# Moving the prompt's down-projection into the sample's seven block products, in a tuned fp32 encoder kernel

## The chip, the core and the metric

The kernel runs on one core of a Trainium2 chip. A core has a matrix engine (PE; its weight loads are shown apart as PEld), a vector engine (DVE), a scalar engine (ACT), a general engine (POOL) and a queue that issues the transfers (SP). The metric is the device time of one execution in microseconds; the lower, the better. Times are medians of several executions, and one more execution was recorded by the hardware profiler. Names such as L816 are lines of the kernel before, unless the text says that they are the changed kernel's.

## The reference, cut to what matters

Two batches go through one encoder layer with the same weights: a prompt of 512 tokens and a sample of 1024 tokens, both 1024 wide.

```python
h = rmsnorm(x, norm_attn_g)
z = h @ w_in                              # q, k, v and the two halves of a gated convolution
a_out = window_attention(q, k, v, bias, sink)          # |q - k| <= 128, 8 heads in 2 groups
c = silu(layernorm(dwconv31(ca * sigmoid(cb))))
x = x + concat(a_out, c) @ w_out
h = rmsnorm(x, norm_ffn_g)
u = dwconv3(h @ w_up)                     # 1024 -> 2 * 2816
x = x + (silu(u[..., :2816]) * u[..., 2816:]) @ w_down # 2816 -> 1024
y = rmsnorm(x, norm_final_g)
```

In the attention, with a sink logit `sk` for each head, `m = max(max(sc), sk)`, `p = exp(sc - m)` and the denominator is `sum(p) + exp(sk - m)`.

## The kernel before

Everything is fp32. A matmul operand is split in two rounded parts, `hi = round(x)` by a cast on ACT and `lo = x - hi` by a subtraction on POOL or DVE, and a product is made of three matmuls: hi·hi, hi·lo and lo·hi. So one "matmul of the algorithm" is three of the profile, nearly all of them 128x128 weights against 512 columns.

The program is emitted as one long list and then ordered by a scheduler that replays it against its own timeline; for each engine the result is one fixed order. What stands beside what is set while emitting: a main line of projections calls `tick()` after a few matmuls, and `tick()` advances two side queues by rates. `side` holds generators for the attention and the output projection (rates `RA` to `RE`), `convs` and `late` hold the taps of the 31-wide convolution, 0.66 credits each (rates `CA`, `CB`, `CL`, `CLO`, `CD`). From the last step of the sample's up-projection on, PE and SP are ordered by hand: they run in the order of the program text.

The stages, in order of time:

1. The prompt's and the sample's input projections (L250 to L253), with the prompt's attention, its convolution and its output projection (L641 to L643) from the side queues, to about 350 us.
2. The prompt's feed-forward layer in 22 steps of 128 hidden channels each (`ffn_step`). A step makes the gate half and the value half (8 chunks of three matmuls each, L250 to L253, 48 matmuls), evacuates them with ACT (L779) and two three-tap passes on DVE each (L775), and gates them: tanh on ACT (L793), `(t + 1) * a` on DVE (L794), times the value on DVE or POOL (L795), then the split (L797, L798). Every second step the down-projection `down` of two steps runs: for 4 token tiles and 2 column halves, six matmuls (L813 to L815) and an addition into the residual on DVE (L816). `w_down` is loaded (L750) and split (L143, L144) for this. Beside it, `side` runs the whole attention of the sample (16 units of four heads: scores L502, reduction L505, softmax L512 to L519, transposes L546, values L560 and L561), and `late` runs the sample's convolution (L293).
3. The sample's output projection (L641 to L643) and the sums for the next stage.
4. The sample's up-projection as a block algorithm with seven products instead of eight (Winograd's form of Strassen's): tokens, channels and columns are cut in halves, L1045 to L1047. The gated values of each pair of hidden blocks and their sums go to DRAM, seven tensors `ga[i, p]` for each of 11 pairs `p` (L1183 to L1198).
5. The sample's down-projection by the same seven products, `ORDER = (1, 2, 5, 6, 7, 4, 3)`: a product `i` is summed over the 11 pairs; a step loads `ga[i, p]` and a block of `w_down` (L1308), forms the block's difference, splits both, and runs 12 matmuls (4 token tiles, L1354 to L1356) into two wide banks of PSUM of 128x1024. At the end of a product the banks are evacuated and combined (`evacuate`). The last product is cut so that its tiles finish one after another (`finish`: sum of squares on ACT, reciprocal root on POOL, scale and store).

PSUM has four wide banks in stage 5, so that with two for each product the next product begins in the other two.

## Time and profile before

| | before |
|---|---|
| median of 3 runs | 1562.63 us (1561.66 to 1564.55) |
| the profiled execution | 1563.92 us, span 1562.1 us |
| PE busy in the span | 1519.2 us, 6909 matmuls and transposes |
| DVE busy | 1200.5 us |
| ACT busy | 799.2 us |
| POOL busy | 729.5 us |
| moved by DMA | 207.62 MB, 133 GB/s |

"Busy" is the time in which an instruction of the engine was under way. The matmuls of PE overlap: one lasts some 0.39 us, and the next starts 0.23 us after it. A view by windows gives the busy time of each engine in a stretch of the span, with the number of instructions behind an x. A view by groups gives the count, the total and the mean in ns of one instruction of a line, then the idle time of the engine just ahead of them and what ended it.

### The profile page before, as it was taken

The numbers are of one execution on the slowest core, as the hardware profiler recorded it, in microseconds if no ns is written. First come the engines' busy times: TensorE is split into PE (matmuls) and PEld (weight loads), VectorE is DVE, ScalarE is ACT, GpSimd is POOL, SyncE is SP. The second block draws the span as 40 slices with busy tenths as digits, with TensorE's granted clock in tenths as the row PEclk, the third lists the DMA queues.
The fourth block names the chain that finished last, engine by engine and source line by source line (L and its number), as shares of the span: only waits on it lengthen the run. The fifth ranks groups of instructions, "written<-read, shape, count | busy, mean of one in ns | idle before, by whom it ended". The sixth has DMA issues, their size and how long they took to land. (4 is left out here: it accounts for less than half of the span.)

```text
span 1562.1 us, 20200 instructions
## 1 busy us (share of the span) xinstructions
PE 1519.2 (97%) x6909; PEld 1234.5 (79%) x6909; DVE 1200.5 (77%) x1731; ACT 799.2 (51%) x1426; POOL 729.5 (47%) x559
## 2 busy tenths in 40 slices
PE   8899899999998999999999999999999999999998
PEld 6787788887886778888877887888888878788886
DVE  7999868638989996756675768777777777877795
ACT  4634566335565655656554455444444445544364
POOL 7651344238576676656653324555555554000135
PEclk9999999999999999999999999999999999999999
DMA  7573246446331333333657222333333332694642
GB/s 229 157 201 95 87 118 165 130 133 166 108 117 64 108 108 109 99 97 95 212 164 230 82 68 78 111 102 101 101 102 102 101 102 101 206 354 144 219 142 108
DMA packets 209771, 207.62 MB, mean 133 GB/s; under 512 B 11156, under 2 KB 150748, under 8 KB 209541
## 3 DMA queue, kind: packets, MB, share of 16 engines
q1 hardware_dynamic: 209669, 206.35, 42.0%
q8 instruction: 54, 0.88, 0.2%
q14 instruction: 48, 0.39, 0.1%
HBM read 158.84 MB, written 48.51 MB: 133 GB/s over the span
## 5 line engine op out<-in xcount | busy, mean ns | idle before, releaser
L144 POOL TENSOR_TENSOR q<-q,q 128x1024 fp32r<-128x1024 f32 x72 | 175.0, 2436 | 68.8 <-ACT q L143 33.8
L921 POOL TENSOR_TENSOR q<-q,q 128x512 fp32r<-128x512 f32 x82 | 114.0, 1401 | 155.9 <-ACT q L1031 151.4
L250 PE MATMUL u<-h,q 128*128 128x512 f32 x400 | 158.5, 396 | 3.6 <-DVE h L775 2.8
L251 PE MATMUL u<-h,q 128*128 128x512 f32 x400 | 158.6, 396 | 0.6 <-DVE h L212 0.6
L253 PE MATMUL u<-h,q 128*128 128x512 f32 x384 | 151.9, 396 | 2.2 <-POOL q L144 2.2
L1045 PE MATMUL w<-h,q 128*128 128x512 f32 x372 | 147.4, 396 | 3.1 <-ACT h L1126 1.7
L1047 PE MATMUL w<-h,q 128*128 128x512 f32 x372 | 145.9, 392 | 0.6 <-POOL q L921 0.6
L293 DVE SCALAR_TENSOR_TENSOR c<-c,cvw,c 128x512 f32<-128x512 f32 x184 | 138.1, 750 | 2.4
L1046 PE MATMUL w<-h,q 128*128 128x512 f32 x350 | 137.6, 393 | 0.0
L143 ACT CAST q<-q 128x1024 fp32r<-128x1024 f32 x72 | 75.6, 1050 | 77.5 <-POOL q L144 44.6
L918 POOL TENSOR_TENSOR q<-q,q 128x1024 f32<-128x1024 f32 x8 | 23.8, 2989 | 182.9 <-DVE q L918 171.2
L250 PE MATMUL b<-h,q 128*128 128x512 f32 x256 | 102.1, 399 | 2.9 <-DVE d L323 2.9
L1354 PE MATMUL w<-h,h 128*128 128x512 f32 x264 | 103.8, 393 | 0.0
L1356 PE MATMUL w<-h,h 128*128 128x512 f32 x264 | 103.6, 392 | 0.0
L921 DVE TENSOR_TENSOR h<-h,h 128x512 fp32r<-128x512 f32 (+1 forms) x128 | 92.3, 764 | 11.4 <-ACT h L925 9.2
L251 PE MATMUL b<-h,q 128*128 128x512 f32 x256 | 100.7, 393 | 0.0
L253 PE MATMUL b<-h,q 128*128 128x512 f32 x256 | 100.5, 393 | 0.0
L1355 PE MATMUL w<-h,h 128*128 128x512 f32 x244 | 95.9, 393 | 0.0
L921 POOL TENSOR_TENSOR c<-q,c 128x512 fp32r<-128x512 f32 x46 | 71.0, 1557 | 51.8 <-ACT c L1031 51.8
L250 PEld LDWEIGHTS u<-h,q 128*128 128x128 f32 x400 | 75.6, 189 | 20.4 <-DVE h L775 3.3
L925 ACT CAST h<-h 128x512 fp32r<-128x512 f32 x101 | 58.7, 618 | 59.4 <-DVE h L921 27.0
L251 PEld LDWEIGHTS u<-h,q 128*128 128x128 f32 x400 | 75.5, 189 | 16.4 <-DVE h L212 1.6
(457 smaller groups left out, 4278.8 us busy)
## 6 DMA issues: line engine op xcount, KB each, us to landing
q<-in_w_up SPq DMA_DIRECT2D x88, 512.0 KB
h<-in_w_down SPq DMA_DIRECT2D x90, 256.0 KB
ga<-q SPq DMA_DIRECT2D x64, 256.0 KB
h<-ga SPq DMA_DIRECT2D x57, 256.0 KB
q<-in_w_in SPq DMA_DIRECT2D x28, 512.0 KB
q<-in_x_sample SPq DMA_DIRECT2D x15, 512.0 KB
h<-qsd SPq DMA_DIRECT2D x24, 256.0 KB
q<-ga SPq DMA_DIRECT2D x20, 256.0 KB
```

The lines of the kernel that those rows point to most:

```text
L144: (nc.vector if dve else nc.gpsimd).tensor_tensor(lo[:], raw[:], hi[:].bitcast(F32), op=ALU.subtract)
L250: nc.tensor.matmul(out, whi[:, kc, :], hi[:], start=(kc == 0), stop=False)
L251: nc.tensor.matmul(out, whi[:, kc, :], lo[:], start=False, stop=False)
L253: nc.tensor.matmul(out, wlo[:, kc, :], hi[:], start=False, stop=(kc == KC - 1))
L293: nc.vector.scalar_tensor_tensor(acc[:], src(t), w(t), acc[:], op0=ALU.mult, op1=ALU.add)
L921: (eng or nc.vector).tensor_tensor(out, a, b, op=ALU.subtract)
L1045: nc.tensor.matmul(out, whi[:, s], hi[:], start=(start and c == 0), stop=False, **go)
L1046: nc.tensor.matmul(out, whi[:, s], lo[:], start=False, stop=False, **go)
L1047: nc.tensor.matmul(out, wlo[:, s], hi[:], start=False, stop=(stop and c == 3), **go)
L1354: nc.tensor.matmul(out, sh[:, c], th[:], start=(p == 0), stop=False)
L1355: nc.tensor.matmul(out, sh[:, c], tl[:], start=False, stop=False)
L1356: nc.tensor.matmul(out, sl[:, c], th[:], start=False, stop=(p == NPAIR - 1))
```

## The change

The prompt's down-projection no longer runs inside stage 2. `ffn_step` ends with `gate`, which writes the gated values of the prompt to DRAM in the form that the seven products need: tokens in two halves of 256, hidden blocks in pairs, seven tensors `gb[i, p // 2]` that hold two pairs each. For that it makes four sums of 128x256 for each pair, three on DVE and one on POOL, and 17 of the 22 products with the value half are on POOL (6 before). `w_down` is neither loaded nor split in stage 2, and there is no addition into the residual; the residual of the prompt goes to DRAM (`x1d`, four more tensors).

In stage 5 a step now serves six token tiles: the four of the sample and two of the prompt (`w = 2`), against the same split block of `w_down`. There are three wide banks for each product, `trio` instead of `pair2`, and the order within a product runs its first two and its last two pairs bank by bank. The last product runs the prompt's tiles along with the sample's first two; the prompt's four output blocks are finished there.

The softmax works on negated scores: the reduction (L505) yields `-(sc + bias)` and its minimum, begun from `-sk`, so that the two small DVE operations after it (L512, L513) are gone; the exponentials take scale -1, and the sink's exponential is made for one head at a time on ACT.

The rates of the side queues are other ones (`RD`, `RN`, `CL`, `CLO`, `CD`), and the sample's attention is queued at step 1 instead of step 3 (`U0`).

```diff
-RA, RB, RBO, RD, RN, RE = 1.2, 0.8, 2.5, 0.52, 0.8, 0.9
+RA, RB, RBO, RD, RN, RE = 1.2, 0.8, 2.5, 0.78, 0.95, 0.9
-CL, CLO, CD = 0.5, 0.6, 0.65
+CL, CLO, CD = 0.7, 0.7, 0.6
-U0 = 3
+U0 = 1
...
-                out=p[:, :nk], in0=sc[:, :nk], in1=bias[h][:, off:off + nk], scale=1.0,
-                scalar=-3.0e38, op0=ALU.add, op1=ALU.max, accum_out=mx[:, j:j + 1])
+                out=p[:, :nk], in0=sc[:, :nk], in1=bias[h][:, off:off + nk], scale=-1.0,
+                scalar=nsink[:, h:h + 1], op0=ALU.add, op1=ALU.min, accum_out=negm[:, j:j + 1])
...
-        nc.vector.scalar_tensor_tensor(negm[:], mx[:], -1.0, nsink[:, hs], op0=ALU.mult, op1=ALU.min)
-        nc.vector.tensor_tensor(es[:], sinkb[:, hs], negm[:], op=ALU.add)
         for j in range(GRP):
-            nc.scalar.activation(pr[j][:, :nk], pr[j][:, :nk], AF.Exp, bias=negm[:, j:j + 1],
+            nc.scalar.activation(pr[j][:, :nk], pr[j][:, :nk], AF.Exp, scale=-1.0, bias=negm[:, j:j + 1],
                                  accum_out=den[:, j:j + 1])
-        nc.scalar.activation(es[:], es[:], AF.Exp)
+        for j in range(GRP):
+            h = kv * GRP + j
+            nc.scalar.activation(es[:, j:j + 1], sinkb[:, h:h + 1], AF.Exp, bias=negm[:, j:j + 1])
...
+    def gate(j, a, b):
+        t = sb.tile([NT])
+        nc.scalar.activation(t[:], a[:], AF.Tanh, scale=0.5)
+        nc.vector.scalar_tensor_tensor(t[:], t[:], 1.0, a[:], op0=ALU.add, op1=ALU.mult)
+        (nc.vector if j % 4 == VG else nc.gpsimd).tensor_tensor(t[:], t[:], b[:], op=ALU.mult)
+        p = j // 2
+        if j % 2 == 0:
+            even_p[p] = t
+            store_gb(1, p, t[:, HL])
+            return
+        e, x, y = even_p.pop(p), sb.tile([NT]), sb.tile([HT])
+        store_gb(2, p, t[:, HL])
+        store_gb(4, p, t[:, HR])
+        eng = nc.vector
+        eng.tensor_tensor(x[:, HR], e[:, HR], t[:, HR], op=ALU.add)
+        store_gb(5, p, x[:, HR])
+        nc.gpsimd.tensor_tensor(x[:, HL], e[:, HL], e[:, HR], op=ALU.subtract)
+        store_gb(7, p, x[:, HL])
+        eng.tensor_tensor(e[:, HR], x[:, HR], e[:, HL], op=ALU.subtract)
+        store_gb(6, p, e[:, HR])
+        eng.tensor_tensor(y[:], t[:, HL], e[:, HR], op=ALU.subtract)
+        store_gb(3, p, y[:])
...
+        if p % 2 == 0:
+            g = pr.pop((("g", i, 0), p // 2))
+            n = slice(0, min(2, NPAIR - p) * HT)
+            hi, lo = hp[i, p // 2] = sb.tile([NT], F32R), sb.tile([NT], F32R)
+            nc.scalar.copy(hi[:, n], g[:, n])
+            sub(lo[:, n], g[:, n], hi[:, n].bitcast(F32))
...
     def mm_down(out, i, p, tt):
         (sh, sl), (th, tl) = hl[i, p]
-        c = slice(tt * P, (tt + 1) * P)
+        if tt < 4:
+            c = slice(tt * P, (tt + 1) * P)
+        else:
+            sh, sl = hp[i, p // 2]
+            c0 = (p % 2) * HT + (tt - 4) * P
+            c = slice(c0, c0 + P)
...
+    def group(i, p, w, lead=LEAD):
+
+        k = ORDER.index(i) * NPAIR + p
+        if len(pr) < CAP and sum(f[0][0] == "h" for f in sb.free) > ROOM:
+            load_next(1)
+        make(k + lead)
+        if w not in pd:
+            pd[w] = wide()
+        for q in range(2):
+            mm_down(pd[w][:, q * NT:(q + 1) * NT], i, p, 2 * w + q)
...
+    def product(i):
+        rest = [(p, w) for p in range(2, NPAIR - 2) for w in range(NW3)]
+        if i == 1:
+            order = [(1, 0), (1, 1), (0, 2), (1, 2)]
+        else:
+            order = [(p, w) for w in range(NW3) for p in range(2)]
+        order += rest + [(p, w) for w in range(NW3) for p in (NPAIR - 2, NPAIR - 1)]
+        for p, w in order:
+            group(i, p, w)
...
+    done_at = {1: 4, 3: 5, 4: 0, 6: 1, 7: 2, 9: 3}
+    for p, w in [(0, 2), (1, 2), (0, 0), (1, 0)] + [(p, w) for p in range(2, NPAIR) for w in (2, 0)]:
+        last_group(p, w)
+        if w == 0 and p in done_at:
+            tt = done_at[p]
+            finish(4 + tt if tt < 4 else tt - 6, (cut(u, tt), cut(e, tt)), False)
+    for tt in (4, 5, 0, 1):
+        add(cut(o12, tt), zs[tt // 2][:, (tt % 2) * NT:(tt % 2 + 1) * NT], cut(o12, tt))
+        finish(tt if tt < 4 else tt - 8, (cut(o11, tt), cut(o12, tt)), False)
```

How the order of the engines changes is shown at three places. A row is an instruction with its line, what it writes and reads, and the shape that it writes; the letter ahead of a tile's number is its kind of buffer (h 128x512 and q 128x1024 in SBUF, c a padded convolution row or the convolution's PSUM bank, s small, and a, b, u, w banks of PSUM).

First, DVE in the middle of the feed-forward layer. Before, in one step (L775 the three-tap passes, L816 the additions of the down-projection, L293 convolution taps, of which only the first of a run is shown, L549 splits of transposed attention weights, L794 and L795 the gate):

```order
L775 SCALAR_TENSOR_TENSOR h_741_4510<-u_228_4460,fw,h_741_4510 128x511
L549 TENSOR_TENSOR h_740_4499<-a_230_4493,h_739_4498 128x512
L816 TENSOR_TENSOR q_476_2841<-b_234_4591,q_476_2841 128x512
L293 SCALAR_TENSOR_TENSOR c_235_4600<-c_479_2906,cvw,c_235_4600 128x512
L816 TENSOR_TENSOR q_476_2841<-b_236_4610,q_476_2841 128x512
L775 SCALAR_TENSOR_TENSOR h_752_4573<-u_232_4530,fw,h_752_4573 128x511
L794 SCALAR_TENSOR_TENSOR h_756_4583<-h_756_4583,h_741_4510 128x512
L795 TENSOR_TENSOR h_756_4583<-h_756_4583,h_752_4573 128x512
L570 TENSOR_TENSOR h_761_4605<-a_231_4502,h_735_4468 64x512
L816 TENSOR_TENSOR q_478_2885<-b_237_4620,q_478_2885 128x512
```

The changed kernel, in an odd step (its L762 are the passes, L791 the product with the value half, L801, L805 and L807 the sums, L292 the convolution, L548 and L524 of the attention):

```order
L762 SCALAR_TENSOR_TENSOR h_765_4785<-u_243_4723,fw,h_765_4785 128x511
L292 SCALAR_TENSOR_TENSOR c_244_4731<-c_473_2930,cvw,c_244_4731 128x512
L791 TENSOR_TENSOR h_769_4795<-h_769_4795,h_765_4785 128x512
L548 TENSOR_TENSOR h_781_4878<-a_251_4872,h_780_4877 128x512
L801 TENSOR_TENSOR h_770_4799<-h_744_4648,h_769_4795 128x256
L524 TENSOR_SCALAR h_763_4778<-h_763_4778,s_761_4773 128x384
L805 TENSOR_TENSOR h_744_4648<-h_770_4799,h_744_4648 128x256
L762 SCALAR_TENSOR_TENSOR h_782_4889<-u_247_4813,fw,h_782_4889 128x511
L807 TENSOR_TENSOR h_771_4800<-h_769_4795,h_744_4648 128x256
```

The additions into the residual, one input from PSUM, are gone; the sums, both inputs from SBUF, stand in their place, three for every second step.

Second, ACT at one unit of the sample's attention. Before (L515 exponentials of a head, L517 the sink's, L548 casts, L285 products for the convolution, L779 the evacuation of a half):

```order
L515 ACTIVATE h_767_4638,s_765_4633<-h_767_4638,s_764_4632 128x384
L515 ACTIVATE h_768_4643,s_765_4633<-h_768_4643,s_764_4632 128x384
L515 ACTIVATE h_770_4669,s_765_4633<-h_770_4669,s_764_4632 128x384
L515 ACTIVATE h_771_4674,s_765_4633<-h_771_4674,s_764_4632 128x384
L285 ACTIVATE h_782_4786<-c_479_2906,cvw 128x512
L779 ACTIVATE h_783_4791<-u_248_4733,vecs,fw 128x512
L517 ACTIVATE s_766_4634<-s_766_4634 128x4
```

The changed kernel (its L512 are the exponentials, L516 the sink's, one for each head, L789 a tanh, L142 the cast of a `w_up` chunk):

```order
L512 ACTIVATE h_763_4778,s_761_4773<-h_763_4778,s_760_4772 128x384
L516 ACTIVATE s_762_4774<-sinkb,s_760_4772 128x1
L512 ACTIVATE h_773_4824,s_761_4773<-h_773_4824,s_760_4772 128x384
L789 ACTIVATE h_769_4795<-h_752_4715 128x512
L284 ACTIVATE h_806_5034<-c_473_2930,cvw 128x512
L142 CAST q_793_4959<-q_772_4811 128x1024
L766 ACTIVATE h_765_4785<-u_243_4723,vecs,fw 128x512
L512 ACTIVATE h_764_4783,s_761_4773<-h_764_4783,s_760_4772 128x384
```

An exponential now waits for its own head's reduction alone, and four small instructions stand where there was one.

Third, PE where one product of stage 5 ends and the next begins, one row for the six matmuls of a step into one bank, its first (the line that multiplies hi by hi). Before, banks 45 and 46 belong to one product and 47 and 48 to the next:

```order
L1354 MATMUL w_45_12145<-h_1886_12364,h_1884_12360 128x512
L1354 MATMUL w_46_12146<-h_1886_12364,h_1884_12360 128x512
L1354 MATMUL w_47_12504<-h_1893_12390,h_1891_12386 128x512
L1354 MATMUL w_48_12505<-h_1893_12390,h_1891_12386 128x512
L1354 MATMUL w_47_12504<-h_1900_12416,h_1898_12412 128x512
```

The changed kernel, with three banks for each product:

```order
L1318 MATMUL w_51_12054<-h_1868_12243,h_1866_12239 128x512
L1318 MATMUL w_52_12078<-h_1863_12214,h_1861_12210 128x512
L1318 MATMUL w_52_12078<-h_1868_12243,h_1866_12239 128x512
L1318 MATMUL w_53_12091<-h_1863_12214,h_1857_12183 128x512
L1318 MATMUL w_53_12091<-h_1868_12243,h_1870_12247 128x512
L1318 MATMUL w_54_12422<-h_1876_12278,h_1874_12274 128x512
L1318 MATMUL w_54_12422<-h_1883_12311,h_1881_12307 128x512
L1318 MATMUL w_55_12448<-h_1876_12278,h_1874_12274 128x512
```

Before, each step went through both banks of its product. Now the last two steps of a product, and the first two of the next, go bank by bank: between the last matmul into bank 51 and the first into 55, the first that can need 51's place, stand three runs of twelve matmuls. The weights of the third bank (`h_1857`, `h_1870`) are the prompt's.

262 lines of the change are left out of this document (94 added, 168 removed).

## Prediction

> **What bounds the kernel now.** I read the page first: spans, busy times, slices.
>
> ```profile
> span 1562.1 us, 20200 instructions
> PE 1519.2 (97%) x6909; PEld 1234.5 (79%) x6909; DVE 1200.5 (77%) x1731; ACT 799.2 (51%) x1426; POOL 729.5 (47%) x559
> PE   8899899999998999999999999999999999999998
> DVE  7999868638989996756675768777777777877795
> ```
>
> PE is busy almost throughout, so what counts is how many matmuls there are and where PE still idles. DVE has a full stretch in slices 9 to 15, the first half of the prompt's feed-forward layer. Next, the view by windows: start and end, length, busy PE, PEld, DVE, ACT and POOL with their instructions, clock, DMA share, GB/s.
>
> ```profile
> 150.00:200.00 50.00, 44.97 (x217) 35.76 (x216) 42.68 (x88) 31.19 (x74) 16.93 (x12) 1.00 0.30 90
> 350.00:450.00 100.00, 97.53 (x449) 78.93 (x448) 88.07 (x147) 57.29 (x102) 71.33 (x45) 1.00 0.44 126
> 450.00:630.00 180.00, 171.79 (x784) 138.93 (x783) 159.50 (x284) 106.83 (x204) 118.31 (x77) 0.99 0.33 104
> 630.00:775.00 145.00, 145.00 (x686) 120.11 (x684) 97.11 (x175) 82.83 (x164) 87.53 (x56) 1.00 0.39 121
> 775.00:830.00 55.00, 51.38 (x230) 40.16 (x229) 36.12 (x53) 26.47 (x56) 27.49 (x36) 1.00 0.65 206
> 1325.00:1355.00 30.00, 27.71 (x120) 21.96 (x119) 28.64 (x37) 19.19 (x29) 0.84 (x1) 1.00 0.51 171
> 1355.00:1550.00 195.00, 195.00 (x848) 158.93 (x847) 145.62 (x198) 90.24 (x166) 38.01 (x32) 1.00 0.58 201
> ```
>
> From 1355 to 1550 PE never idles, and 848 matmuls take 195 us: a matmul of 512 columns costs 0.230 us of PE's time. The 0.39 us that the groups give for one overlaps with its neighbours and is no price. Between 350 and 630 PE idles 10.7 us by these rows, while DVE is busy for 247.6 of 280; after 630 DVE is at 67% and PE's idle time is gone. So the first half of that layer is bound by DVE and PE together, the last stage by PE alone.
>
> How close DVE is to its limit there follows from the timeline, at the first matmul of step 0 and of step 14 and at DVE's first pass of step 0 and of step 11:
>
> ```profile
> 350.62 0.44 PE L250 MATMUL u<-h,q 128*128 128x512 f32 x1
> 626.20 0.40 PE L250 MATMUL u<-h,q 128*128 128x512 f32 x1
> 361.74 0.74 DVE L775 SCALAR_TENSOR_TENSOR h<-u,fw,h 128x511 f32<-128x511 f32 x1
> 580.99 0.74 DVE L775 SCALAR_TENSOR_TENSOR h<-u,fw,h 128x511 f32<-128x511 f32 x1
> ```
>
> In the order of the program, 342 DVE instructions stand between those two passes; each kind at its mean from the rows below (and for the small kinds their own) they sum to 218 us, and the stretch took 219.3. DVE was full. PE's 1210 instructions of steps 0 to 13, at 0.23 us for 512 columns and in proportion for fewer, sum to 257 us; the stretch took 275.6. So PE lost 18.7 us there, some of it hidden in the overlap that the windows count as busy.
>
> **PE's own work.** The prompt's down-projection is 22 blocks x 4 tiles x 2 halves x 3 = 528 matmuls. As seven products it is 7 x 11 pairs x 2 tiles x 3 = 462, and the order shows nothing else that PE gains or loses. 66 matmuls x 0.230 us = **15.2 us less**, in stages where PE is the bound: 121 us leave the feed-forward layer, 106 us arrive in the last stage.
>
> **DVE in the feed-forward layer**, the term that decides how much is left of it. The rows by group (count, total in us, mean ns, idle before):
>
> ```profile
> L816 DVE TENSOR_TENSOR q<-b,q 128x512 f32<-128x512 f32 x88 | 59.9, 685 | 19.4 <-PE b L815 18.8
> L795 DVE TENSOR_TENSOR h<-h,h 128x512 f32<-128x512 f32 x16 | 18.1, 1134 | 0.2
> L775 DVE SCALAR_TENSOR_TENSOR h<-u,fw,h 128x511 f32<-128x511 f32 x88 | 65.4, 744 | 13.8 <-ACT h L779 13.2
> L794 DVE SCALAR_TENSOR_TENSOR h<-h,h 128x512 f32<-128x512 f32 x22 | 24.4, 1111 | 2.8 <-ACT h L793 2.4 <-issue 0.2
> L293 DVE SCALAR_TENSOR_TENSOR c<-c,cvw,c 128x512 f32<-128x512 f32 x184 | 138.1, 750 | 2.4
> L505 DVE CUSTOM_DVE_ANT_0 h<-a,h 128x384 f32<-128x384 f32 x57 | 30.5, 551 | 22.5 <-PE a L502 12.4 <-DMA catd<-h 4.4 <-PE a L561 2.9
> L549 DVE TENSOR_TENSOR h<-a,h 128x512 fp32r<-128x512 f32 x42 | 28.5, 682 | 5.2 <-ACT h L548 5.1
> L362 DVE TENSOR_TENSOR q<-b,q 128x256 fp32r<-128x256 f32 x4 | 1.7, 420 | 1.6 <-ACT q L361 1.6
> L512 DVE SCALAR_TENSOR_TENSOR s<-s,nsink x24: 138/163/2186, 122.2 to 747.9; 128x4 f32<-128x4 f32 x24
> L513 DVE TENSOR_TENSOR s<-sinkb,s 128x4 f32<-128x4 f32 x24 | 13.0, 543 | 0.2
> ```
>
> Gone are 59.9 us of additions, 11 of the 16 gate products (12.5 us) and L512 and L513. New are 33 sums of 128x256. No row has that form with both inputs in SBUF: below, the 0.42 us of L362, one input in PSUM; above, 1.13 us, L795 at twice the width. I take 0.85 us: L795 lies 0.45 us above L816, which has one input in PSUM, and even the four columns of L512 took from 0.14 to 2.19 us, so the surplus looks like a wait that doesn't shrink with the width.
>
> The Trainium skill, SBUF — State Buffer, section Who interferes with whom, says that a DVE instruction with two SBUF inputs contends with a POOL instruction that reads SBUF and that the one that comes second is blocked until the other is through. The trace agrees (L795 against L816, 1134 and 685 ns), and the rule speaks against this change, which puts two-input sums in the place of additions from PSUM. Without it, at 0.42 us, DVE would have 10 us less up to step 16, and the time would be near 1535 us.
>
> In the changed order the last tap of the sample's convolution stands in step 15, so steps 0 to 15 are the full stretch now. DVE's instructions there: 92 taps and 9 other convolution rows 75.6 us, 64 passes 47.6, 16 gates 17.8, 54 reductions with their reads 33.4, 39 splits 26.6, 24 sums 20.4, 13 rows of L570's kind 8.9, normalisation and denominators 16, four products 4.5: **251 us**. PE's 1140 instructions there sum to **231.6 us**. DVE thus passes step 16 at 361.7 + 252 = 614 us, and PE's first matmul of a step leads DVE's first pass by 11.1 us (step 0) to 23.1 (step 11, 557.9 and 581.0): PE comes to step 16 between 591 and 603 us, where its own work would bring it to 582. That is 9 to 21 us of idle PE, and I take 15 against the 18.7 of before: **3.7 us less**. Below, no idle time at all, 18.7 less. Above: ACT's share rises, since the same softmax, casts and evacuations stand in shorter steps (202 us of 247 by its rows, 141 of 219 before), so DVE may wait more; at 6% more, 252 becomes 267 and PE idles 30 to 36 us, **up to 17 more** than before. After step 16 a step has 13 us of PE and 8 to 10 of DVE, so nothing is lost there, as after 630 us now.
>
> POOL and ACT lose the splits of `w_down` and of the gated values, 66 casts and as many subtractions less, and POOL gains 11 products and 11 sums. They lie beside PE both ways (POOL 118 of 180 us busy between 450 and 630): nothing on the path.
>
> **Softmax.** ACT's exponentials wait for L512:
>
> ```profile
> L515 ACT ACTIVATE h<-h,s 128x384 f32<-128x384 f32 (+1 forms) x92 | 52.5, 573 | 35.0 <-DVE s L512 34.7
> L517 ACT ACTIVATE s<-s 128x4 f32<-128x4 f32 x24 | 4.6, 193 | 0.7 <-DVE s L513 0.7
> ```
>
> The wait now ends at the head's own reduction; a unit saves 0.59 + 0.54 us of DVE and pays 3 x 0.19 us of ACT. What the sums above don't hold is the prompt's attention, where PE idles 5.0 us (150 to 200): I take **1.5 us less**, between 5 less and none. That the reduction costs the same with scale -1 and a start value from SBUF is assumed; at the 0.75 us of a tap instead of 0.55 it would put 11 us on DVE, inside the upper bound above.
>
> **The seams.** At 775 to 830 PE idles 3.6 us while the output projection starts, although some 20 us of the down-projection's matmuls (29 in each of three lines, by the order) still stand there. They are gone; the new order puts the first half-projection's attention rows ahead instead. I take **1 us more**, between 3 less and 8 more. In the last stage the first product needs a third bank, which the last hidden block's gate half leaves:
>
> ```profile
> L1162 ACT ACTIVATE q<-w,vecs,fw 128x1024 f32<-128x1024 f32 x26 | 31.4, 1207 | 25.5 <-PE w L1047 23.1 <-DMA ga<-q 0.9 <-DVE w L918 0.8
> L1163 DVE SCALAR_TENSOR_TENSOR q<-w,fw,q 128x1023 f32<-128x1023 f32 x26 | 33.3, 1282 | 44.4 <-ACT q L1162 44.4
> L1421 POOL TENSOR_TENSOR q<-q,q 128x512 f32<-128x512 f32 x6 | 8.5, 1444 | 0.0
> ```
>
> One evacuation and two passes are 3.8 us, and 24 matmuls (5.5 us) cover them if DVE comes at once; 28.6 of 30 us busy says that it may not: **1 us more** (0 to 3). At a later boundary 36 matmuls (8.3 us) stand before a bank is needed again, for one evacuation of 1.2 us: nothing. At the end four blocks are finished instead of two while the last 66 matmuls run (15.2 us); POOL has some 2.8 us for each, L1421 included, 11.2 together: **0.5 us more** (0 to 2).
>
> The last stage otherwise: 42 splits more put 26 us on ACT and 29 on DVE, where DVE had 145.6 of 195 us, and 106 us of PE come with them. Transfers: 77 stores of 128 KB and as many bytes back, against 11.5 MB of `w_down` less; the last stage moves 39 MB in 195 us now, and would move some 51 in 300. Hidden.
>
> **Sum.** -15.2 - 3.7 - 1.5 + 1 + 1 + 0.5 = -17.9 us against the profiled 1563.9 (span 1562.1 and 1.8 around it): 1546. That execution was 1.3 us above the median, so **1545 us**.
>
> **The rivals.** (1) *DVE keeps up*: PE's idle time in steps 0 to 15 goes altogether, since DVE's surplus over PE falls from 26 us (218 against 192 in steps 0 to 10) to 19 and PE starts 11 us ahead. 18.7 instead of 3.7: 1530 us. Against it: in those steps before, DVE was full and PE lost time. (2) *The layer becomes bound by DVE and ACT together*: with three engines at 80 to 100%, in order, each delay is passed on. At 13 more instead of 3.7 less: 1562 us. For it: ACT's share; against it: DVE lost only 1.3 us of 219 before. (3) *The seam*: the output projection waits for its convolution rows, now that no matmuls cover them; 8 us: 1552. (4) *Slower: SP holds up the weights*. SP issues in order, and in each odd step the stores of the sums stand ahead of `w_up` loads.
>
> ```profile
> SPq L1188 <- DVE q L1183: 69.8, 11, 26.4
> ```
>
> Stores of the same kind already wait up to 26.4 us for DVE in the next stage. A chunk is loaded about one and a half steps (some 22 us) ahead and needs 1.05 us of cast and 2.4 of POOL first; once a store waits over some 15 us, PE waits for weights. At 3 us for each of 11 pairs: 33 us, 1578. Against it: in the stage of that row PE loses no time.
>
> **Chances.** Forecast 0.50 (alone 1536 to 1555), rival 1 0.17, rival 2 0.15, rival 3 0.11, rival 4 0.07. The range leaves out half of rival 1 and of rival 2 and all of rival 4, some two in ten: **1531 to 1560**. A measurement of this kernel tells 0.2% (3.1 us) from no change. Rivals 1 and 3 and the forecast are faster; of rival 2 about half is, a third is the same and the rest slower: faster 0.85, same 0.05, slower 0.10.
>
> **What would show it.** PE with 6843 matmuls and transposes and about 16 us less busy; PE idle between steps 0 and 15 of the layer near 15 us with DVE at 95% or more; step 21 of the layer beginning near 662 us (350.6, the 296.6 that the order's matmuls of steps 0 to 20 sum to, and 15); sums near 0.85 us; no idle PE at the product boundaries. Sums at 0.42 us or an idle-free layer would speak for rival 1; PE waiting for POOL's split behind a `w_up` load for rival 4. A time over 1560 would mean that DVE's stretch grew and the step "15 against 18.7" was wrong.

## The result: slower by 16.7 us

| | before | changed |
|---|---|---|
| median | 1563.59 us | 1580.29 us |
| ratio | | 1.0107 (95%: 1.0090 to 1.0125) |
| profiled execution, span | 1563.92, 1562.1 us | 1580.89, 1579.1 us |
| matmuls and transposes | 6909 | 6843 |

The forecast was 1545 us (1531 to 1560), so the kernel came out 35 us above it and on the other side of the kernel before. The page of the changed kernel, spans and busy times and three rows of the slices (40 slices of 39.5 us):

```profile
span 1579.1 us, 20219 instructions
PE 1519.8 (96%) x6843; PEld 1237.4 (78%) x6843; DVE 1211.3 (77%) x1661; ACT 805.3 (51%) x1476; POOL 687.1 (44%) x525
PE   8999998997998998999999999999999999999997
DVE  7999865765989999775686787788786945668883
PEclk9999998997999999999999999999999999999999
```

There are 66 matmuls less, and PE is busy for as long as before (1519.2). The row PEclk says why: in the seventh and the tenth slice, where the kernel before had a 9, the clock granted to PE is lower, and a matmul takes longer. The same by windows, the kernel before first, then the changed one (start and end, length, busy PE, PEld, DVE, ACT, POOL with their instructions, clock, DMA share, GB/s):

```profile
200.00:265.00 65.00, 65.00 (x322) 54.06 (x321) 46.26 (x90) 39.46 (x81) 31.75 (x26) 1.00 0.57 146
350.00:400.00 50.00, 47.53 (x219) 37.82 (x218) 45.42 (x68) 27.96 (x41) 38.69 (x24) 1.00 0.60 167
400.00:700.00 300.00, 291.79 (x1342) 238.35 (x1341) 248.09 (x447) 172.84 (x339) 192.83 (x123) 0.99 0.32 100
```

```profile
200.00:265.00 65.00, 59.51 (x274) 47.87 (x273) 42.47 (x80) 35.94 (x80) 27.95 (x23) 0.92 0.48 122
350.00:400.00 50.00, 40.61 (x165) 32.47 (x164) 28.41 (x57) 27.16 (x61) 28.62 (x19) 0.83 0.67 174
400.00:700.00 300.00, 282.30 (x1300) 230.48 (x1300) 275.48 (x448) 200.87 (x404) 199.78 (x124) 0.97 0.49 150
1250.00:1300.00 50.00, 49.48 (x216) 40.23 (x215) 29.95 (x42) 21.38 (x33) 0.00 (x0) 1.00 0.68 242
1300.00:1560.00 260.00, 260.00 (x1129) 211.97 (x1128) 178.89 (x220) 106.99 (x198) 59.19 (x46) 1.00 0.47 157
```

In the same 50 us at the start of the layer PE does 165 matmuls instead of 219; in the last stage it does 1129 in 260 us, 0.230 us each, as forecast.

Busy time hides such losses, since a slow matmul counts as busy. So in what follows PE's **lost time** is used: for each matmul, the time until the next one starts, less the pitch that its size has where nothing hinders it (0.229 us for 512 columns, 0.174 for 384, 0.117 for 256, 0.108 for a transpose). It holds waits and slow clock together:

| us lost by PE | before | changed | difference |
|---|---|---|---|
| 0 to 200 | 25.1 | 22.4 | -2.7 |
| 200 to 350, second half of the input projection | 0.9 | 10.7 | +9.8 |
| 350 to 400, start of the feed-forward layer | 4.0 | 17.3 | +13.3 |
| 400 to 900, layer and output projection | 22.4 | 34.5 | +12.1 |
| 900 to the last matmul | 11.1 | 7.7 | -3.4 |
| from the last matmul's end to the end | 7.2 | 10.0 | +2.8 |
| 66 matmuls of 0.229 | | | -15.1 |

That sums to 16.8 of the 17.0 us between the two spans. The matmuls were saved as predicted; 35 us came back in three places ahead of 900 us.

**How a wait is paid twice.** Some of the first matmuls of step 0's value half in the changed kernel, start and duration:

```profile
388.70 0.77 PE L249 MATMUL u<-h,q 128*128 128x512 f32 x1 [1.90 <-DVE h L762]
389.26 0.63 PE L250 MATMUL u<-h,q 128*128 128x512 f32 x1
389.69 0.63 PE L252 MATMUL u<-h,q 128*128 128x512 f32 x1
393.40 0.39 PE L252 MATMUL u<-h,q 128*128 128x512 f32 x1
393.63 0.39 PE L249 MATMUL u<-h,q 128*128 128x512 f32 x1
```

After a wait of 1.9 us they start 0.43 us apart (0.56 us behind the first), and from 393.4 on 0.23 us. Windows laid on the clock's steps, all three in the changed kernel, show what was granted:

```profile
246.50:256.70 10.20, 7.43 (x20) 5.57 (x20) 8.49 (x16) 6.19 (x13) 3.36 (x5) 0.50 0.57 121
383.00:393.20 10.20, 7.59 (x20) 5.90 (x21) 8.42 (x23) 8.99 (x29) 6.03 (x5) 0.50 0.27 66
673.10:679.90 6.80, 5.67 (x13) 4.47 (x14) 4.71 (x7) 4.10 (x8) 3.76 (x3) 0.50 0.87 253
```

Between the first 20 us and the last 25, PE runs at half clock for 3.4 us before and for 44.4 us in the changed kernel, in seven stretches. Of the time lost from 200 to 830 us, matmuls that began at half clock make up 1.5 us before and 16.3 now, and all else, waits in the main, 25.0 and 44.1: 19 us of new waiting brought 15 us of slow matmuls. The Trainium skill, TensorE: Matmul & The Clock Gate, Part 1: The HAM clock gate, describes this: PE's clock is halved after an idle window of about 3.4 us and given back after a busy one. The lengths agree (3.4, 6.8 and 10.2 us); how idle the window must be differs, see the last section.

### The profile page after: what moved, and what is told of

Read it like the earlier page. It is cut to its first block, busy times and chain, and to the rows that moved or that the text cites. A ratio compares the mean times of both kernels' runs of the same rounds, so it can differ in the third digit from the quotient of the medians.

```text
span 1579.1 us, 20219 instructions
## 1 busy us (share of the span) xinstructions
PE 1519.8 (96%) x6843; PEld 1237.4 (78%) x6843; DVE 1211.3 (77%) x1661; ACT 805.3 (51%) x1476; POOL 687.1 (44%) x525
## 5 line engine op out<-in xcount | busy, mean ns | idle before, releaser
L866 DVE TENSOR_TENSOR h<-h,h 128x512 fp32r<-128x512 f32 (+2 forms) x202 | 156.0, 804 | 65.4 <-ACT h L870 25.1
L1318 PE MATMUL w<-h,h 128*128 128x512 f32 x462 | 181.4, 393 | 0.5 <-DVE q L1108 0.5
L1320 PE MATMUL w<-h,h 128*128 128x512 f32 x462 | 181.7, 393 | 0.0
L1319 PE MATMUL w<-h,h 128*128 128x512 f32 x462 | 181.5, 393 | 0.0
L249 PE MATMUL u<-h,q 128*128 128x512 f32 x400 | 165.2, 414 | 10.7 <-DVE h L762 7.9
L250 PE MATMUL u<-h,q 128*128 128x512 f32 x400 | 162.7, 407 | 0.0
L252 PE MATMUL u<-h,q 128*128 128x512 f32 x384 | 155.0, 404 | 1.2 <-POOL q L143 1.2
L292 DVE SCALAR_TENSOR_TENSOR c<-c,cvw,c 128x512 f32<-128x512 f32 x184 | 137.6, 748 | 2.1
L863 POOL TENSOR_TENSOR q<-q,q 128x1024 f32<-128x1024 f32 x12 | 33.2, 2774 | 236.0 <-DVE q L863 219.6
L870 ACT CAST h<-h 128x512 fp32r<-128x512 f32 x120 | 72.0, 619 | 93.7 <-DVE h L866 41.7
L249 PE MATMUL b<-h,q 128*128 128x512 f32 x256 | 102.7, 401 | 2.5 <-DVE d L322 1.6
L1318 PEld LDWEIGHTS w<-h,h 128*128 128x128 f32 x462 | 86.9, 188 | 20.5 <-ACT h L870 0.9
L249 PEld LDWEIGHTS u<-h,q 128*128 128x128 f32 x400 | 78.3, 196 | 31.1 <-DVE h L762 4.2
L142 ACT CAST q<-q 128x1024 fp32r<-128x1024 f32 x72 | 75.1, 1046 | 53.7 <-DMA q<-in_w_in 16.7
L1319 PEld LDWEIGHTS w<-h,h 128*128 128x128 f32 x462 | 86.8, 188 | 19.7
L1320 PEld LDWEIGHTS w<-h,h 128*128 128x128 f32 x462 | 86.8, 188 | 19.5
L252 PE MATMUL b<-h,q 128*128 128x512 f32 x256 | 101.8, 398 | 0.0
```

The lines of the kernel that those rows point to most:

```text
L249: nc.tensor.matmul(out, whi[:, kc, :], hi[:], start=(kc == 0), stop=False)
L250: nc.tensor.matmul(out, whi[:, kc, :], lo[:], start=False, stop=False)
L252: nc.tensor.matmul(out, wlo[:, kc, :], hi[:], start=False, stop=(kc == KC - 1))
L292: nc.vector.scalar_tensor_tensor(acc[:], src(t), w(t), acc[:], op0=ALU.mult, op1=ALU.add)
L866: (eng or nc.vector).tensor_tensor(out, a, b, op=ALU.subtract)
L1318: nc.tensor.matmul(out, sh[:, c], th[:], start=(p == 0), stop=False)
```

## The experiments

All times are medians, against the kernel before in the same series (1563.6 to 1566.2 us). "Lost" is PE's lost time in the stretches of the table above; "half" the us at half clock.

| run | us | ratio to before (95%) | lost 200-350 | 350-400 | 400-900 | half |
|---|---|---|---|---|---|---|
| before | 1563.6 | 1 | 0.9 | 4.0 | 22.4 | 3.4 |
| changed | 1580.3 | 1.0107 (1.0090-1.0125) | 10.7 | 17.3 | 34.5 | 44.4 |
| e1_conv_rates | 1578.6 | 1.0097 (1.0079-1.0114) | 11.2 | 13.3 | 37.2 | 37.5 |
| e2_u0 | 1585.1 | 1.0148 (1.0124-1.0171) | 10.0 | 16.9 | 37.2 | 44.4 |
| e3_both | 1588.4 | 1.0167 (1.0148-1.0186) | 11.1 | 13.5 | 48.2 | 58.0 |
| e4_softmax_alone | 1575.7 | 1.0078 (1.0061-1.0095) | 11.4 | 6.0 | 23.8 | 23.9 |
| f1_one_bank | 1596.4 | 1.0202 (1.0179-1.0225) | 9.8 | 11.3 | 53.4 | 51.2 |
| f2_sums_on_pool | 1591.4 | 1.0170 (1.0147-1.0193) | 11.6 | 11.1 | 52.4 | 51.2 |
| f3_old_softmax | 1572.5 | 1.0043 (1.0023-1.0063) | 3.6 | 12.1 | 34.5 | 23.9 |
| f4_old_softmax_pool | 1600.2 | 1.0228 (1.0207-1.0248) | 3.8 | 9.9 | 61.6 | 47.8 |
| g1_filler | 1660.7 | 1.0622 (1.0591-1.0654) | 10.1 | 5.4 | 10.0 | 17.1 |
| h1_late_stores | 1572.9 | 1.0058 (1.0038-1.0077) | 11.2 | 4.3 | 40.5 | 27.3 |
| h2_late_stores_old_softmax | 1569.2 | 1.0042 (1.0026-1.0058) | 3.9 | 4.7 | 38.0 | 23.9 |
| i1_two_units_ahead | 1585.0 | 1.0130 (1.0105-1.0154) | 3.8 | 8.3 | 56.8 | 44.4 |
| j1_late_stores_gb | 1584.4 | 1.0118 (1.0092-1.0145) | 10.5 | 5.7 | 45.8 | 37.5 |
| j2_gb_old_softmax | 1573.2 | 1.0051 (1.0034-1.0068) | 5.6 | 4.8 | 41.2 | 34.1 |
| j3_gb_sums_on_pool | 1572.1 | 1.0043 (1.0029-1.0056) | 4.2 | 4.3 | 39.8 | 20.5 |
| j4_gb_old_rates | 1576.8 | 1.0065 (1.0043-1.0087) | 0.9 | 4.4 | 48.9 | 27.3 |
| k1_quarter_filler | 1610.5 | 1.0293 (1.0273-1.0314) | 11.8 | 5.1 | 46.6 | 41.0 |
| k2_filler_on_best | 1576.3 | 1.0071 (1.0048-1.0093) | 3.8 | 3.6 | 20.1 | 3.4 |

One thing holds for all of them: the scheduler orders the whole list anew after every edit, so that an edit moves work far from its own place too. What an edit does is therefore read in its own stretch first, and differences of a few us elsewhere are not put down to it.

### Is it the rates?

```diff
-CL, CLO, CD = 0.7, 0.7, 0.6        # e1, e3
+CL, CLO, CD = 0.5, 0.6, 0.6
-U0 = 1                             # e2, e3
+U0 = 3
```

> The changed kernel with the convolution's old rates (CL 0.5, CLO 0.6); all else as changed. Theory A (the order's new rates put the waits where they are): the 10 us that PE lost more than before between 200 and 350 us go, since the taps no longer stand in rows of two to six on DVE while the prompt's attention and convolution normalisation wait there; some taps move to the next layer's full DVE stretch and cost 2 us: 1572 us, between 1569 and 1574. Theory B (with the down-projection's matmuls gone, PE has nothing to fill a wait of DVE with, whatever the rates): the taps come back as idle PE in the layer: 1577 to 1583 us.

> The changed kernel with the sample's attention queued at step 3 again (U0 = 3). Theory A: the 13 us that PE loses in the first 50 us of the layer (29 us for step 0 against 17 before) shrink to about 5, as the transfers of q, k and the scores no longer stand between the first weights and the first steps; the attention ends later, which costs 2: 1574 us, between 1571 and 1577. Theory B: the delay only moves on, since the DVE work of the layer is the same and has two steps less to lie in: 1579 us or more.

> Both of the preceding edits: CL 0.5, CLO 0.6, U0 = 3, with the seven products and the new softmax as changed. Theory A: the gains add: 1564 to 1568 us, at or near the kernel before. Theory B: 1577 us or more. Half way between (1572) would say that both hold.

Not these rates. With the old `CL` and `CLO` 200 to 350 loses as much as in the changed kernel (11.2 and 10.7), and the time is level with it; `U0` only pushes the loss out to the end of the layer (in e2_u0 20.8 us between 700 and 900), and both together are 8 us slower than the changed kernel. With `U0 = 3` a score still waits 2.3 us for Q at 367.6, inside step 0. `RD`, `RN` and `CD` kept their new values in every run, so that their part is not known.

### The softmax

e4 makes the softmax edit alone in the kernel before, f3 takes it back in the changed one (the diff is that of the change, read one way or the other).

> The kernel before with the softmax on negated scores alone (its old down-projection, rates and queue). If this part does what the prediction said: 1.5 us less, 1562 us (1559 to 1564). A rival in which the four small exponentials on ACT or the reduction with a start value from SBUF cost more than they save: 1567 us or more, with the reduction's mean above 0.6 us.

> The changed kernel with the softmax of before (two small DVE operations after the reduction, one sink exponential for four heads), all else as changed. If the softmax costs here what it cost alone, 12 us: 1568 us, with the 10 us lost between 225 and 260 gone. Rival: in a layer bound by DVE the 14 us of DVE that the new softmax saves are worth more than its order costs: 1580 to 1590 us, the loss at 225 to 260 gone and a larger one between 400 and 700.

Alone it costs 12 us, and taking it back gains 7.8. Both times the 200 to 350 column moves (0.9 to 11.4; 10.7 to 3.6). There, in the changed kernel, PE waits for the last unit of the prompt's attention and the convolution's rows behind it (PE and what it waited for, us, times, longest):

```profile
PE a L559 <- ACT q L547: 2.2, 1, 2.2
PE a L604 <- DMA d<-cvd: 1.9, 1, 1.9
```

and then runs at half clock for 10.2 us. The edit's own prices, in e4_softmax_alone by groups:

```profile
L504 DVE CUSTOM_DVE_ANT_0 h<-a,h,nsink 128x384 f32<-128x384 f32 x57 | 34.3, 611 | 16.9 <-PE a L501 7.5 <-PE a L561 4.2 <-DMA catd<-h 3.7
L518 DVE TENSOR_TENSOR s<-s,s 128x4 f32<-128x4 f32 x24 | 14.1, 586 | 1.5 <-ACT s L517 1.3
L517 ACT ACTIVATE s<-sinkb,s 128x1 f32<-128x1 f32 x96 | 27.1, 283 | 0.0
```

The reduction is 60 ns dearer (551 before), the addition to the denominator takes 586 ns instead of 279, and ACT spends 27.1 us on sink exponentials instead of 4.6. In sum DVE still has 10.8 us less to do than in the kernel before (1189.7 and 1200.5 us busy), and ACT 16.0 more at 52% of the span. So the 12 us are not these prices added up; 10.5 of them stand in the one stretch. From 225 to 265 PE waits there for the convolution's rows (2.8 us), a cast (1.7) and a split (0.7), where the kernel before has no such wait, and runs at half clock for 10.2 us: in the new order these pieces come too close behind what makes them.

### Filler: what the down-projection's matmuls were for

f1 leaves the sample's attention the `a` banks alone, as in the kernel before; g1 adds 480 matmuls that feed nothing, in the bank that the down-projection had; k1 a quarter of them; k2 a quarter on the best variant.

```diff
-    use.update(attn="ab")
+    use.update(attn="a")                     # f1, g1, k1
...
         gate(k, ug[0], uv[0])
+        if k in range(1, 21, 2):             # g1: 8 times; k1: 2 times; k2: once in each step 0 to 19, "ab"
+            for d in range(8):
+                pd = banks.tile([NT], among="b")
+                for m in range(6):
+                    nc.tensor.matmul(pd[:], upw[k + 1, 0][0][:, m, :], h2[0, 0][m][0][:], start=(m == 0), stop=(m == 5))
```

> The changed kernel with the sample's attention in its own banks alone (`attn` "a" as before, not "ab"). With the old rates the layer still began with 9 to 11 us of lost PE time, and always ahead of scores (L500) into a `b` bank that the down-projection no longer fills. If the free `b` banks are what brings scores in front of step 0: the 17 us lost between 350 and 400 become 4 to 8, 1570 us (1566 to 1574). Rival: the scores wait for DVE wherever they stand, and the loss moves on into the layer: 1577 us or more.

> f1_one_bank (1596 us) with 480 matmuls of 128x512 that feed nothing, put behind the gate of every second step into a `b` bank, nearly as many as the old down-projection had in the layer (528); the output is unchanged. By the pitch of 0.230 us they are 110 us of PE. If the down-projection's matmuls were what hid the layer's waits (the filler theory): of the 62 us that PE loses between 350 and 700 in f1_one_bank, 30 to 40 go, and the time is 1666 to 1676 us. Rival, the waits come from the order and the transfers alone and stay: 1700 to 1706 us.

> g1_filler with a quarter of the dose: f1_one_bank (1596 us) with 12 idle matmuls behind every second step, 120 or 27.6 us of PE in all. g1_filler paid 64 us for 110. If the first matmuls do the most (they end the idle stretches and keep the clock up): 1590 to 1600 us, no dearer than none. If filler hides only in proportion to its size (4 us of each 10): 1612 us. If nothing: 1624 us.

> h2_late_stores_old_softmax (1569 us, PE loses 39 us from 350 to 700) with 6 idle matmuls in each of the steps 0 to 19, again 120 or 27.6 us. Here less is lost, so less can be hidden: 1570 to 1578 us if they fall into waits, 1585 in proportion to g1_filler, 1597 us if they hide nothing.

f1 came out 26 us above its first expectation: with fewer banks the start of the layer loses 6 us less, but the layer behind it 19 us more, so the free `b` banks help. The layer in f1_one_bank, then in g1_filler:

```profile
350.00:400.00 50.00, 42.27 (x197) 33.87 (x195) 31.24 (x61) 29.02 (x60) 29.27 (x19) 0.93 0.79 204
400.00:725.00 325.00, 293.17 (x1326) 236.81 (x1325) 265.87 (x455) 202.62 (x414) 198.86 (x127) 0.95 0.45 140
```

```profile
350.00:400.00 50.00, 45.76 (x222) 37.24 (x221) 32.22 (x58) 28.07 (x58) 29.51 (x19) 1.00 0.76 207
400.00:725.00 325.00, 325.00 (x1535) 270.57 (x1534) 227.18 (x421) 191.04 (x387) 174.03 (x109) 1.00 0.38 116
```

With filler PE never idles from 400 to 725 and the clock stays at 1.00; 110 us of matmuls cost 64, 5 us below the expected range. The other 46 us had been lost time: 64.7 us from 350 to 900 in f1, 15.4 in g1. A quarter of the filler (27.6 us) costs 14.1 us on f1, so that it hides in proportion and its first matmuls do no more than the rest, and 7.1 on h2, where it takes the losses from 350 to 900 from 42.7 to 23.7 us and the half clock from 23.9 to 3.4.

So the layer has room for matmuls that wait for nothing: they cost a quarter to six tenths of their length there, shown three times. That the 528 matmuls of the old down-projection filled the same room is what this suggests; it was not tried by taking them out of the kernel before alone. Taking 121 us of them out of the layer saved 121 less the 25.4 us that 350 to 900 lost more. Not all of the 25.4 is missing cover: 13.3 of them stand in 350 to 400, the first matmul of the old down-projection came at 380 us, and h1 below takes these 13 away without filler, though 6 of them come back behind 400. Nor does filler say what PE waits for; it would hide the waits of short chains and those for a full engine alike.

### Is DVE the bound of the layer?

```diff
-VG = 3
+VG = 9                              # no gate product on DVE
-        eng = nc.vector
+        eng = nc.gpsimd             # f2 and f4 with attn="a"; f4 with the softmax of before
```

> f1_one_bank, and in addition DVE relieved: the three sums of each pair and the gate products of every fourth step on POOL, so that 33 sums and 5 products (some 30 us by their groups) leave DVE in the layer. If the layer is bound by DVE, of which PE has nothing to hide: PE's losses between 400 and 700 (31 us) fall by 15 to 25, 1550 us (1545 to 1558). Rival, POOL is then the one that is late (its splits of w_up wait behind the sums): no gain or a loss against f1_one_bank, with PE waiting for POOL's splits.

> f2_sums_on_pool with the softmax of before. If the two gains are independent: 12 us below f2_sums_on_pool, near 1540 us, better than both kernels. If DVE is what counts, 5 us or more above f2_sums_on_pool.

With one bank for the attention, no. From 400 to 650 DVE falls from 215.4 of 250 us in f1 to 197.0 in f2, 79%, and PE's losses in 400 to 900 stay (53.4 and 52.4); of the 5 us that f2 gained, 1 stands there. In f2 PE waits there for DVE and DVE for PE, in turn:

```profile
DVE h L503 <- PE a L500: 29.9, 20, 3.3
PE u L249 <- DVE h L762: 7.0, 3, 4.3
PE a L545 <- DVE s L503: 6.0, 7, 1.4
PE a L500 <- DVE h L569: 5.4, 4, 3.2
```

These are the links of one chain (scores, reduction, exponential, transposes, values), each in the fixed order of its engine. None of the engines is full in f2; each waits for the others' last piece. f4, where the old softmax should have added its gain, lost 9 us on f2 instead, all of it between 400 and 700. Its expectation had called such a loss a sign that DVE counts, but DVE is busy for less in f4 (1167.6 us) than in f2 (1176.3), so it is none.

With two banks, as in the changed kernel, the question is open. There DVE is busy for 94.5% of the time from 390 to 640, and every wait of PE that the profile names from 400 to 700, 17.6 us in all, ends with DVE. The two longest groups:

```profile
PE u L249 <- DVE h L762: 6.0, 5, 3.1
PE a L545 <- DVE h L524: 3.9, 2, 3.4
```

j3 (below) takes the same work off DVE as f2, from j2. From 390 to 640 DVE falls from 232.8 to 223.2 us, and steps 0 to 15 take PE 248.1 us instead of 257.3. Steps 16 to 20 took 6 us more, and the median gained 1.1 us. So there DVE's work does seem to set the length of the first steps, though relieving it by way of POOL gained next to nothing in sum.

### The start of the layer, and SP

```diff
-            nc.sync.dma_start(x1d[i][:], x[:])          # h1, h2: for the prompt behind steps 2 to 5
...
-            x1.pop(k)                                   # with the residual kept until then
...
-        nc.sync.dma_start(gb[i, p // 2][:, p % 2, :], src)
+        owed.append((i, p, src[0], src[1]))             # j1 to j4: issued in the next step
```

> The changed kernel with the prompt's four residual stores (x1d, 512 KB each) issued in steps 2 to 5 of the layer instead of right behind the output projection, where SP stands between 328 and 349 us and waits for the last additions with the loads of K, V, bias and w_up behind it. If these stores hold up the start of the layer: the 17 us lost between 350 and 400 become 6 to 10, 1571 us (1568 to 1574). Rival, the scores are held up by DVE and the two softmax chains, not by transfers: 1578 us or more.

> h1_late_stores with the softmax of before. If the stores and the softmax are two causes of their own: 1562 to 1565 us (1572 of f3_old_softmax less 8 to 10), level with the kernel before. Rival: the stores matter little, 1570 us or more.

h1 gained 7.4 us, and the start of the layer lost 4.3 us instead of 17.3 (400 to 900 lost 6.0 more), but not by the mechanism that was expected. The scheduler issued the stores as early as ever (first the changed kernel, then h1; SP's issues and waits):

```profile
328.49 2.62 SPq L648 DMA_DIRECT2D x1d<-q  x2
373.99 0.38 SPq L136 DMA_DIRECT2D q<-in_w_up  x1
374.47 2.46 SPq L677 DMA_DIRECT2D q<-ksd  x4
...
SPq L136 <- PE a L208: 11.1, 1, 11.1
PE b L500 <- DMA q<-ksd: 2.5, 2, 1.5
PE b L500 <- DMA h<-qsd: 2.5, 1, 2.5
```

```profile
329.32 2.62 SPq L853 DMA_DIRECT2D x1d<-q  x2
358.65 2.41 SPq L679 DMA_DIRECT2D q<-ksd  x4
368.70 2.01 SPq L679 DMA_DIRECT2D q<-ksd  x3
PE a L501 <- DMA q<-ksd: 0.4, 1, 0.4
```

What the edit did change is how long the residual's SBUF slots are held, and so which slots the next loads get. In the changed kernel a load of `w_up` stood 11.1 us on SP until the transposes of the layer's input (L208) had read its slot, with four loads of K behind it. Those transposes stood on PE behind a score that waited 2.5 us for Q, and at 381 and 383 us two scores (L500) waited 2.5 us for that K: in part PE waited for itself by way of SP. In h1 that wait of SP is gone, and the last loads of K are issued at 368.7 instead of 374.5. That the slots alone do this was not tried apart. With the old softmax as well, h2 is the best variant of the change: 1569.2 us, between the two expectations and still slower than the kernel before (ratio 1.0042).

> h2_late_stores_old_softmax with the sample's scores two units ahead of the values instead of one, so that more work lies between a score and what needs its softmax. If PE waits in the layer because each piece stands too near behind the one that it depends on: PE's losses from 400 to 700 (30 us in f3_old_softmax) fall by 8 to 15, 1552 to 1557 us, below both kernels. Rival, DVE is simply full: the same as h2_late_stores_old_softmax within 3 us, or slower.

```diff
-            if u + 1 < u1:
-                yield from scores(u + 1)
+            if u + 2 < u1:          # the sample's attention alone, on h2
+                yield from scores(u + 2)
```

Instead of the gain that was expected it is 16 us slower than h2, and 400 to 900 loses 56.8 us instead of 38.0. More scores in flight made more waits, not fewer.

> h1_late_stores (1573 us) with the stores of the gated values and their sums (gb) issued one step later, when the sums are long done, so that SP doesn't stand in front of them. In the changed kernel SP waits some 90 us of the layer's 350 at these stores (47 for POOL's product alone, 8.4 the longest), with loads of w_up, w_out and the concatenated rows behind it. If that order is a cause of its own (the prediction's fourth rival): PE's losses between 400 and 700 fall by 6 to 12, above all at 590 to 680: 1561 to 1567 us. Rival, the losses come from the chains of the attention alone: 1570 us or more.

> h2_late_stores_old_softmax (1569 us) with the gb stores one step later; the 7.2 us in which PE waits for the concatenated rows at 652 us, while SP stands 7.2 us before gb stores, should go, and the slow clock after it: 1557 to 1561 us. Rival: another wait takes its place: 1566 us or more.

> j2_gb_old_softmax with all sums and all gate products on POOL. With the stores late nothing waits for the sums any more, so POOL may be slow with them, and some 35 us leave DVE: if DVE's load still counts, 5 to 8 us below j2_gb_old_softmax; if the layer's losses are only chains and transfers, the same within 3 us; if POOL's splits of w_up are delayed, slower.

> j2_gb_old_softmax with the convolution's old rates (CL 0.5, CLO 0.6): takes the 3 us lost at 246 and what the taps cost there: 1 to 3 us below j2_gb_old_softmax; if the taps then lengthen the layer, 2 to 5 us above it.

These say little on the fourth rival, since here too the scheduler took the stores forward: SP's waits at them from 385 to 700 fell from 131 us to 117 (h1 to j1) and from 107 to 81 (h2 to j2), and the times rose by 11.5 and 4.0 us. In j2 the wait of 7.2 us for the concatenated rows went as expected, and one of 12.9 us for a three-tap pass took its place at 653 us. Whether SP's stores cost anything in the layer stays open. j3 is level with j2; its profiled execution lies 4.5 us below its median and that of j2 2.0 above, so the 9 us of steps 0 to 15 may be chance in part. j4 removed the loss at 200 to 350 altogether (0.9) and lost 7.7 us more in the layer, where the convolution's taps then stood.

## Why the prediction was wrong

**Right.** The matmuls (6843, 0.230 us, 15.1 us saved). DVE's work in the layer: from its first pass of step 0 (385.4) to that of step 16 (641.4) it took 256 us against 252 forecast, at 94.5% busy (236.4 of the 250 us from 390 to 640). In part that is luck: the working adds up whole durations, and neighbours on DVE overlap a little. By busy time DVE had 202.2 of the 219.3 us in the stretch of the kernel before that the working calls full, and 241.5 of 255.9 here, so it was not quite full in either. The price of the sums in the mean, 0.91 us against 0.85:

```profile
L801 DVE TENSOR_TENSOR h<-h,h 128x256 f32<-128x256 f32 x11 | 13.0, 1180 | 1.4 <-POOL h L791 1.2
L805 DVE TENSOR_TENSOR h<-h,h 128x256 f32<-128x256 f32 x11 | 9.4, 852 | 0.2
L807 DVE TENSOR_TENSOR h<-h,h 128x256 f32<-128x256 f32 x11 | 7.7, 703 | 0.1
```

That the mean was right is luck: the forecast gave each sum the same wait, and in truth most have none and a few have a long one (last section). The product boundaries: 49.5 of 50 us busy at 1250, and the last stage lost 3.4 us less than before.

**Wrong: "I take 15 against the 18.7 of before".** This is the step that failed, by 25 us. The first matmuls of steps 0 and 16, the first DVE passes of the same steps, and the stretch between:

```profile
359.97 0.73 PE L249 MATMUL u<-h,q 128*128 128x512 f32 x2 [1.95 <-ACT h L210]
631.69 0.39 PE L249 MATMUL u<-h,q 128*128 128x512 f32 x1
385.42 1.40 DVE L762 SCALAR_TENSOR_TENSOR h<-u,fw,h 128x511 f32<-128x511 f32 x2
641.36 1.54 DVE L762 SCALAR_TENSOR_TENSOR h<-u,fw,h 128x511 f32<-128x511 f32 x2 [0.79 <-ACT h L766]
390.00:640.00 250.00, 235.38 (x1090) 192.27 (x1090) 236.37 (x406) 170.40 (x354) 164.85 (x103) 0.97 0.42 130
```

From step 0 to step 16 PE took 271.7 us for 231.6 of its own work, so it lost 40 and not 15. With the 9.4 us by which it came late to step 0 and 6 more in steps 16 to 20, step 21 began at 702.98 instead of 662. What was wrong in the step:

- The start, 14 of the 25 us by the working's own terms. It let DVE begin 11.1 us behind PE's step 0, as in the kernel before. DVE began 25.4 us behind it, since PE lost 17 us in 350 to 400, where the kernel before lost 4. h1, with DVE 12.6 us behind, lost 32.7 us in steps 0 to 15, and h2, with 10.4 and the old softmax, 26.8: the start is worth at least 7 of the 25, and even a start as forecast doesn't bring 15.
- The other 11 us. DVE's stretch was 4 us longer than forecast, and PE came to step 16 with a lead of 9.7 us, where the 15 stand for one of 16.5. The sign that the forecast named for a time over 1560, a DVE stretch that grew, is thus hardly what happened. Whether these 11 us are chains of short waits, as f1 and f2 show for one bank, or DVE's own work, as j3 suggests for two, stays open.
- It priced the 121 us that leave the layer at their full value, without asking what else those matmuls did. g1, k1 and k2 show that matmuls cost only a part of their length there.
- It gave a wait its own length. Matmuls at half clock lost 15 us more than in the kernel before.

**Wrong: the softmax, "1.5 us less".** Alone it costs 12.1 us. Up to 200 us the changed kernel lost 2.7 us less, within what the forecast gave for the prompt's attention, and the loss came right after it, at 225 to 260, through the new order. The reduction cost 611 ns instead of 551, and a unit paid 0.94 us of ACT instead of 0.57. That such a small edit moves the order was no term of the sum.

**Small.** The tail: 0.5 forecast, 2.8 measured. The last addition (L863) stands 3 us behind the last matmul, since DVE has two other blocks' passes in front of it, one of them at 1.74 us beside POOL:

```profile
1569.78 1.74 DVE L1389 SCALAR_TENSOR_TENSOR q<-q,s,c 128x512 f32<-128x512 f32 x1 [0.80 <-POOL s L1379]
1572.05 0.68 DVE L863 TENSOR_TENSOR q<-w,q 128x512 f32<-128x512 f32 x1
```

**The rivals.** The second, at 1562 us, had the right place and too small a size; its mechanism wanted DVE and ACT nearly full, and by busy time ACT had 176.3 of the 255.9 us, 69%; the 202 us of the working, its durations added up, came out as forecast. The first is out. The seam, the third, cost what the forecast gave it: from 650 to 925 PE lost 1.3 us more than before. The fourth had the right sign, but no wait of PE for a split of `w_up` stands in 400 to 700 of the changed kernel; whether stores that hold up SP delay other transfers was neither shown nor excluded.

What stays open: what PE waits for in the layer with two banks, and whether another order of the same change would beat the kernel before. h2 would have to lose some 6 us less of its 38 in 400 to 900; no variant here did without paying for it.

## What to carry to other kernels

Matmuls that are taken out of a stretch of dependent pieces can be worth less than their length: they were cover for its waits. Before they are moved, count what else is ready there; if nothing is, price the stretch by the waits that come bare, and in this kernel by most of that again for the clock (15 us on 19). And don't take the start of a stretch over from the old order: here the next engine began 14 us later. And where a scheduler orders the program, an edit of a few small instructions can cost more through the order than all its instructions last: run it alone.

## What the runs showed of the hardware

**PE's clock falls after short gaps.** Over the 20 profiles, in steps of 3.413 us laid on the clock's own changes (60 us to the last 25 us, some 8,600 steps that began at full clock), the 109 steps after which the clock was halved had PE busy between 0 and 61% (median 35%), and in all the rest PE was busy for 43% or more. The longest single gap of such a step was as short as 0.57 us; no step with a gap over 1.95 us kept the clock. To get it back took a step at half clock with PE busy for 83% or more; one with 92% still failed. The Trainium skill, TensorE: Matmul & The Clock Gate, Why this matters for your kernels, asks for no gaps over some 3 us; in these runs the busy share of the step tells the two cases apart better than its longest gap, but not fully: between 43 and 61% busy 26 steps lost the clock and 69 kept it.

**A sum has two prices.** Of the 33 sums in the changed kernel those beside which POOL is idle or nearly so take 0.41 to 0.43 us. The long ones have POOL at work beside them for all but 0.3 us or less of their time:

```profile
665.21 3.86 DVE L801 TENSOR_TENSOR h<-h,h 128x256 f32<-128x256 f32 x1 [0.59 <-POOL h L791]
669.11 0.42 DVE L805 TENSOR_TENSOR h<-h,h 128x256 f32<-128x256 f32 x1
670.05 2.59 DVE L807 TENSOR_TENSOR h<-h,h 128x256 f32<-128x256 f32 x1
```

Nine of them lasted 1.4 to 3.9 us, so the mean of 0.91 is one that no sum has. This is what the page cited in the prediction says (the Trainium skill, SBUF — State Buffer, Who interferes with whom): the second comer is held until the other is through. The trace adds that the hold can last longer than one instruction: the first of the three stood through two of POOL in a row (1.29 and 2.39 us by the profile, whose spans on POOL are rough), the second of which began 1.2 us after it. What the forecast missed is that the hold stands in front of everything behind it on DVE: with the two above, 6.5 us, and PE waits 3.1 us for L762 right after.
